# Making S5's parameters in three pieces, after the first token block instead of within it

## The chip, the cores and the metric

The kernel runs on one core of a Trainium2 chip. The metric is the device time of one execution in microseconds (us); smaller is better. Engines are named as the profile names them: PE is TensorE (PEld its weight loads), DVE is VectorE, ACT is ScalarE, POOL is GpSimd, SP is SyncE, which issues nearly all of this kernel's DMAs in the order of its queue.

## What is computed

One inference step of a two-layer recurrent decoder over a prompt of 2048 tokens and 8 single-token samples, model width 1024, all in float32. The first, even layer matters here. It projects the normed input once; some of the columns go to 4 heads of gated linear attention (GLA), the others to 32 groups of a complex-diagonal state space model (S5). Both results are gated, concatenated and projected back. S5's discretised parameters depend on weights alone:

```python
def s5_scan(u, h0_re, h0_im, lam_re, lam_im, log_dt, b_re, b_im, c_re, c_im, d):
    dt = jnp.exp(log_dt)[:, None]
    mag = jnp.exp(lam_re * dt)
    ar, ai = mag * jnp.cos(lam_im * dt), mag * jnp.sin(lam_im * dt)
    den = lam_re * lam_re + lam_im * lam_im
    wr = ((ar - 1.0) * lam_re + ai * lam_im) / den
    wi = (ai * lam_re - (ar - 1.0) * lam_im) / den
    ...
def even_mixer(h, s_gla, s_re, s_im, ...):
    q, k, v, r, lr, u, sg = jnp.split((h @ w_in).astype(f32), _offsets(EVEN_SIZES), axis=-1)
    ...
    o, s_gla_new = gla_chunked(q, k, v, log_a, s_gla.astype(f32))
    o = rmsnorm(o, gla_norm_w).reshape(bsz, L, GLA_V_WIDTH) * jax.nn.silu(r)
    y5, h_re, h_im = s5_scan(u, s_re.astype(f32), ...)
    ...
    out = jnp.concatenate([o, y5], axis=-1).astype(h.dtype) @ w_out
```

The second, odd layer (a gated delta rule) and the final norm follow; the change doesn't touch them.

## The kernel before

Tokens are worked in four blocks of 512 for GLA (the first also holds the 8 samples) and in two halves for S5. For each block GLA runs an entry (transposes, norm, split of the input into a high and a low part), then per head the dense products (`gla_dense`, 6 projections of 128 columns, three passes each), a prefix of decays (`gla_prefix`), a chain over the four chunks (`gla_chain`) with a gate (`gla_gate`), in the first block a sample step (`gla_sample`), and at the end of the block the output projection (`gla_out`), whose sums are added to the residual on VectorE (line 1064). In the first block the weights come as raw rows and are split by ScalarE and GpSimd (lines 319, 320) and stored; later blocks load the stored halves.

S5's preparation runs beside that. `s5_params` (from line 383) loads three small weight rows, transposes them on TensorE, and makes on VectorE with [128, 32] operations (helper on line 389): the angle reduced to a sine and cosine (two ScalarE activations, lines 436 and 437), nine powers of the complex step, three squarings, and the multiples of the angle, 16 fine (`rb`) and 9 coarse (`ra`). All lie in one tile Q of 68 columns for each of 32 groups, stored by one DMA (line 511) to the DRAM tensor s5q. `s5_state` (line 1078) loads the samples' S5 states in 8 steps into the tile hr, transposes each on TensorE into h0s, and stores h0s. `s5_tables` makes one group's tables from its row of s5q (32 times, about 18 us each, small products on VectorE and GpSimd, two products on TensorE) and stores them in DRAM for the S5 stage.

The order on TensorE is written out: `Weave.run` gives each stream its turn by a planned time, the modelled time of TensorE. A stream yields either so many planned us (`yield LAT["far"]`, 8 us) or an event that another stream posts. TensorE executes in that order, whether the data is there or not. The other engines' order is the scheduler's, in which a stream's lead counts. `s5_make` is the stream of S5's preparation, and has no lead, like the dense streams; chains, prefixes and samples have one.

SBUF places are pools that open and close as stacks on two sides. Before the change `start` (S5's parameters) is open on the right side from the first, and `out2`, which holds GLA's Oh and Ol tiles, opens only after it closes. The event "o0", posted with the first Oh and Ol tiles, lets the first block's gates and samples go on. After `out2` the pool `tabs` opens for the tables, then `ext`, with two more residual buffers. The event ("gtail", 0) is posted when the dense products of the first block's four heads are all issued; the output projection of that block and the entry of the second wait for it, the entry also for the last sample's step. The S5 stage itself waits for the end of all GLA chains and for the tables.

A tile's tag names its place, and a tag with one buffer is reused in turn: a new tile waits until the last reader of the old one, a DMA too, is done.

Of the kernel before, what the change touches and what calls it, by code (L numbers as in the profile page):

```python
# [12 lines left out]
F32 = mybir.dt.float32  # L13
# [5 lines left out]
OP = mybir.AluOpType  # L19
# [4 lines left out]
P = 128  # L24
# [3 lines left out]
NSM = 8  # L28
# [12 lines left out]
           inv4=0.837, inv5=0.796, inv6=0.972, chain1=0.972, chain2=0.729, chain3=0.837, split=1.95, sload=2.66,  # L41
           cout=2.25, norm=5.5, load=2, us=3.74, sq=4, out=3.24, entry=9.6, x=1.88, gentry=7.98, make=30, far=8,
           pr=1.5, gate=9, lvl1=4.73, lvl=1.8, gnorm=6.8, scan=2.33, tab=10, entry5=8, glu=3, gelu=1.5, ysum=6)
# [96 lines left out]
def tile_trunk(ctx, tc, A, O):  # L140
# [244 lines left out]
    def s5_params(st):  # L385
# [4 lines left out]

        temps, tiles = {}, []

        def rt(name):
            k = len(temps) % 8
            if k == 0:
                tiles.append(st.tile([P, 8, SG], F32, tag="rt", bufs=2, name="rt"))
            temps[name] = tiles[-1][:, k]
            return temps[name]

        Q = st.tile([P, SG, NQ], F32, tag="Q", name="Q")  # L400
        cut = lambda a, n: Q[:, :, a:a + 2 * n].rearrange("p g (i n) -> p i n g", i=2)
        pw = cut(0, SR + 1)
        ra, rb = cut(RA, 9), cut(RB, 16)
        rows = st.tile([SG, 3, P], F32, tag="rows", name="rows")
        for h in range(2):
# [19 lines left out]
        lre, lim, dtb = prm[:, 0], prm[:, 1], prm[:, 2]  # L425
        th, kk, mag, t0, t1, t2, t3 = [rt(x) for x in ("th", "kk", "mag", "t0", "t1", "t2", "t3")]
        sn, cs, rden, am1 = [rt(x) for x in ("sn", "cs", "rden", "am1")]
        vtt(t0, lre, dtb, OP.mult)
# [51 lines left out]
        x0 = st.tile([P, 7, SG], F32, tag="rows", name="x0")  # L480
        x1 = st.tile([P, 7, SG], F32, tag="x1", name="x1")

# [6 lines left out]

        for r, top in ((rb, 16), (ra, 8)):  # L490
            nc.gpsimd.memset(r[:, 0, 0], 1.0)
            nc.gpsimd.memset(r[:, 1, 0], 0.0)
            at = lambda n: (r[:, 0, n], r[:, 1, n])
            n = 1
            while n < top:
                if n > 1:
                    m = n - 1
                    cb, sb = [x.unsqueeze(1).to_broadcast([P, m, SG]) for x in at(n)]
                    c_, s_ = r[:, 0, 1:n], r[:, 1, 1:n]
                    vtt(x0[:, :m], c_, cb, OP.mult)  # L500
                    vtt(x1[:, :m], s_, sb, OP.mult)
                    vtt(r[:, 0, n + 1:2 * n], x0[:, :m], x1[:, :m], OP.subtract)
                    vtt(x0[:, :m], c_, sb, OP.mult)
                    vtt(x1[:, :m], s_, cb, OP.mult)
                    vtt(r[:, 1, n + 1:2 * n], x0[:, :m], x1[:, :m], OP.add)
                n *= 2
                square((ra[:, 0, 1], ra[:, 1, 1]) if n == 16 else at(n), at(n // 2))
# [818 lines left out]
    def s5_glu(sp, half):  # L1326
# [64 lines left out]
        if ns:  # L1391
# [10 lines left out]
    sp = Phase(tc, "s5", early=("Hh", "Hl", "h0"), entry=("xb", "rr"),  # L1402
               start=("Q", "rt", "rows", "ldt", "ev", "dt", "drow", "prm", "x0", "x1", "h0s", "hr"),
               tabs=("q", "kp", "pp", "v0", "v1", "bx", "by", "cx", "cy", "xx", "xy", "y1", "y2", "dd", "smI", "smC", "smR"),
# [4 lines left out]
    sp.pools["out"] = gp.pools["out"]  # L1409
    sp.open("start", "right")  # L1410
    gp.open("main", "left")
# [81 lines left out]
    def s5_make():  # L1493
        yield LAT["make"]
        yield from s5_params(sp)
        yield from s5_state()
        sp.close("start")
        gp.open("out2", "right")
        sp.pools["out2"] = gp.pools["out2"]
        og_[GBLK[0]] = gla_o()  # L1500
        weave.post("o0")
        sp.open("tabs", "right")
        for g in range(SG):
            yield from s5_tables(sp, g)
        sp.close("tabs")
        gp.open("ext", "right")
        weave.post("tabs")
# [833 lines left out]
```

## Time and profile before

| | us |
|---|---|
| median of 3 runs | 3261.68 (3260.92 to 3266.36) |
| the profiled execution's own time | 3250.56 |
| its span | 3248.8 |
| TensorE busy | 2955.9 (91%) |
| VectorE busy | 2224.4 (68%) |
| ScalarE busy | 1255.7 (39%) |
| GpSimd busy | 995.0 (31%) |
| DMA, queue of SyncE | 57.3% of 16 engines' span |

The profile is one execution; the profiled execution's own time is 11.1 us below the median of the timed runs. The page cuts the span in 40 slices, and from slice 7 on TensorE is busy for nine tenths or nearly so. To see a stage, a table of stretches is read: busy time of each engine in a window, the clock granted to TensorE as a share of 2.4 GHz, and the share of time that the 16 DMA engines were busy. The window less the busy time is idle time, and the list of waits says on which instruction each idle time ended.

### The profile page before, as it was taken

The numbers are of one execution on the slowest core, as the hardware profiler recorded it, in microseconds if no ns is written. First come the engines' busy times: TensorE is split into PE (matmuls) and PEld (weight loads), VectorE is DVE, ScalarE is ACT, GpSimd is POOL, SyncE is SP. The second block draws the span as 40 slices with busy tenths as digits, with TensorE's granted clock in tenths as the row PEclk, the third lists the DMA queues.
The fourth block names the chain that finished last, engine by engine and source line by source line (L and its number), as shares of the span: only waits on it lengthen the run. The fifth ranks groups of instructions, "written<-read, shape, count | busy, mean of one in ns | idle before, by whom it ended". The sixth has DMA issues, their size and how long they took to land.

```text
span 3248.8 us, 53026 instructions
## 1 busy us (share of the span) xinstructions
PE 2955.9 (91%) x18425; PEld 2497.5 (77%) x18425; DVE 2224.4 (68%) x5715; ACT 1255.7 (39%) x3321; POOL 995.0 (31%) x1236
## 2 busy tenths in 40 slices
PE   6888799999999989978988888899998999999998
PEld 5877678777778768877767888877887788787886
DVE  7766556645444546765867888867887678857885
ACT  5443343323323323241134444443444344434442
POOL 6565444322202222240034444431112121211111
PEclk8898899999999999989999999999999999999999
DMA  7565965673483485664466566676444844475446
GB/s 216 190 209 177 297 184 148 190 256 126 136 276 126 133 287 153 200 202 148 155 198 216 172 193 185 190 230 221 139 147 140 270 146 145 125 234 192 141 139 191
DMA packets 398232, 602.96 MB, mean 186 GB/s; under 512 B 62521, under 2 KB 257964, under 8 KB 397828
## 3 DMA queue, kind: packets, MB, share of 16 engines
q1 hardware_dynamic: 394902, 589.98, 57.3%
q0 software_dynamic: 2560, 8.42, 0.9%
q8 instruction: 145, 2.38, 0.3%
q10 hardware_dynamic: 502, 1.17, 0.1%
q14 instruction: 123, 1.01, 0.1%
HBM read 433.31 MB, written 166.34 MB: 185 GB/s over the span
## 4 chain that ended last, share of the span: by engine, by line
PE 35%; DVE 15%; DMA 4%; issue 3%; ACT 2%; POOL 1%; SPq 0%; POOLq 0%; DVEq 0%; ACTq 0%
PE pmm L93 23%; PE prc L93 5%; PE ptp L97 2%; PE pch L93 2%; DVE yc L1692 2%; PE ppo L93 2%; DVE z L1237 1%; DVE z L1247 1%; DVE Hl L649 1%; DMA out<-yt 1%; DMA LB<-md_d 1%; DVE z L1243 1%; DMA whl<-split 1%; DVE z L1238 0%; DVE z L1248 0%
## 5 line engine op out<-in xcount | busy, mean ns | idle before, releaser
L93 PE MATMUL pmm<-Hh,whl 128*128 128x512 f32 (+4 forms) x5200 | 1597.3, 370 | 42.8 <-ACT pre L1682 13.2
L93 PEld LDWEIGHTS pmm<-Hh,whl 128*128 128x128 f32 x5200 | 951.2, 193 | 173.8 <-ACT pre L1682 14.8
L93 PE MATMUL pmm<-Hl,whl 128*128 128x512 f32 (+5 forms) x2640 | 937.0, 355 | 5.6 <-DVE Hl L649 4.2
L93 PEld LDWEIGHTS pmm<-Hl,whl 128*128 128x128 f32 (+1 forms) x2640 | 506.5, 192 | 55.6 <-DVE Hl L649 6.0
L93 PE MATMUL pmm<-Oh,whl 128*128 128x512 f32 (+2 forms) x1120 | 354.3, 379 | 30.5 <-DVE res L1064 13.4
L320 POOL TENSOR_TENSOR whl<-raw,whl 128x512 fp32r<-128x512 f32 (+1 forms) x176 | 232.3, 1322 | 203.9 <-ACT whl L319 194.9
L93 PEld LDWEIGHTS pmm<-Oh,whl 128*128 128x128 f32 x1120 | 211.3, 200 | 65.7 <-DVE res L1064 16.9
L1692 DVE SCALAR_TENSOR_TENSOR yc<-pre,cvec,yc 128x512 f32<-128x512 f32 (+1 forms) x288 | 228.8, 795 | 43.2 <-ACT yc L1690 40.5
L93 PE MATMUL pmm<-Ol,whl 128*128 128x512 f32 (+2 forms) x560 | 203.3, 363 | 0.6 <-DVE Ol L370 0.6
L319 ACT ACTIVATE whl<-raw 128x512 fp32r<-128x512 f32 (+1 forms) x176 | 108.5, 618 | 127.4 <-PE pmm L93 78.0
L93 PEld LDWEIGHTS pmm<-Ol,whl 128*128 128x128 f32 x560 | 112.6, 201 | 11.4 <-DVE Ol L370 1.7
L907 DVE TENSOR_TENSOR dlt<-b 128x512 f32<-128x512 f32 x112 | 87.5, 782 | 39.8 <-ACT E L914 38.9
L93 PE MATMUL pmm<-oh,whl 128*128 128x512 f32 (+3 forms) x320 | 93.6, 370 | 18.3 <-DVE res L1378 15.4
L908 ACT ACTIVATE E<-dlt 128x256 f32<-128x256 f32 x112 | 47.4, 423 | 156.1 <-DVE dlt L907 32.3
L1682 ACT ACTIVATE pre<-pmm 128x512 f32<-128x512 f32 (+1 forms) x120 | 61.1, 510 | 115.4 <-PE pmm L93 115.1
L646 POOL TENSOR_TENSOR xb<-xb,rr 128x1024 f32<-128x1024 f32 (+1 forms) x32 | 76.9, 2412 | 90.9 <-DMA xb<-xs_d 40.4
L1968 ACT ACTIVATE jk<-ppo,rq 128x128 bf16<-128x128 f32 x128 | 46.7, 365 | 140.2 <-PE ppo L93 139.1
L1685 POOL COPY halo<-pre 128x3 f32<-128x3 f32 x96 | 22.3, 232 | 241.0 <-ACT pre L1682 240.3
L1064 DVE TENSOR_TENSOR res<-pmm,res 128x512 f32<-128x512 f32 (+2 forms) x80 | 46.2, 584 | 68.6 <-PE pmm L93 50.0
L1729 ACT ACTIVATE jk<-ptp 128x128 bf16<-128x128 f32 x256 | 70.8, 277 | 53.8 <-PE ptp L97 48.3
L275 POOL TENSOR_TENSOR s<-s,mhalf 128x4 f32<-128x4 f32 (+2 forms) x41 | 40.6, 989 | 162.6 <-DVE s L274 160.7
L1695 ACT ACTIVATE th<-yc 128x512 f32<-128x512 f32 (+1 forms) x96 | 61.0, 635 | 73.1 <-DVE yc L1692 72.8
(1527 smaller groups left out, 6103.8 us busy)
## 6 DMA issues: line engine op xcount, KB each, us to landing
whl<-split SPq DMA_DIRECT2D x460, 512.0 KB
split<-whl SPq DMA_DIRECT2D x168, 512.0 KB
res<-xs_d SPq DMA_DIRECT2D x88, 256.0 KB
sm<-s5m SPq DMA_DIRECT2D x32, 514.0 KB
raw<-in_w_in_even SPq DMA_DIRECT2D x64, 256.0 KB
xs_d<-res SPq DMA_DIRECT2D x64, 256.0 KB
raw<-in_w_in_odd SPq DMA_DIRECT2D x64, 256.0 KB
LB<-md_d SPq DMA_DIRECT2D x64, 256.0 KB
```

What stands on the lines that cost most here:

```text
L93: return self.e.matmul(out, w, x, **kw)
L97: return self.e.transpose(out, x, ident)
L319: nc.scalar.activation(t[:, 0, :m], raw, AF.Copy)
L320: nc.gpsimd.tensor_tensor(t[:, 1, :m], raw, t[:, 0, :m].bitcast(F32), op=OP.subtract)
L646: nc.gpsimd.tensor_tensor(xb, xb, rr.unsqueeze(1).to_broadcast(list(xb.shape)), op=OP.mult)
L907: nc.vector.tensor_tensor(d3, b3, b3[:, :, s - 1:s].to_broadcast([P, nb_, 2 * s]), op=OP.subtract)
L908: nc.scalar.activation(E3[:, :, s:], d3[:, :, s:], AF.Exp, scale=IS)
L1682: nc.scalar.activation(pre[:, X0 + c * P:X0 + (c + k) * P], ps[:, n0:], AF.Copy)
L1692: nc.vector.scalar_tensor_tensor(yv, pre[:, i:W - 3 + i], convw[:, ti, i:i + 1], yv, op0=OP.mult, op1=OP.add)
L1695: nc.scalar.activation(t[:, 3:W], yv, AF.Tanh, scale=0.5)
L1729: nc.scalar.activation(jk, pt[:, c * P:(c + 1) * P], AF.Square, accum_out=ss[:, c:c + 1])
L1968: nc.scalar.activation(jk[:rows], po[:rows, c * P:(c + 1) * P], AF.Square, scale=rq[:rows, c:c + 1], accum_out=s1[:, c:c + 1])
```

## The change

The parameters are no longer made at 30 planned us but when the first block's dense products have been issued, in the place where the tables lie afterwards. `out2` opens at the start of the kernel and "o0" is posted at once. To fit, the tile Q becomes three pieces in two tags, and hr and h0s take the same two tags:

- tag qb: the nine powers (18 columns), then the coarse multiples `ra` (18 columns), then h0s
- tag qa: the loaded weight rows, then the fine multiples `rb` (32 columns), then hr

Each piece is stored by its own DMA to its columns of s5q. The temporaries share one tile, the multiples are made in steps of at most four instead of up to seven, and the last squarings go to `cs` and `sn` and are copied into the pieces.

```diff
     def s5_make():
-        yield LAT["make"]
+        og_[GBLK[0]] = gla_o()
+        weave.post("o0")
+        yield "gtail", 0
+        sp.open("start", "right")
         yield from s5_params(sp)
         yield from s5_state()
         sp.close("start")
-        gp.open("out2", "right")
-        sp.pools["out2"] = gp.pools["out2"]
-        og_[GBLK[0]] = gla_o()
-        weave.post("o0")
         sp.open("tabs", "right")
...
     gp.open("out", "right")
     sp.pools["out"] = gp.pools["out"]
-    sp.open("start", "right")
+    gp.open("out2", "right")
+    sp.pools["out2"] = gp.pools["out2"]
...
     def s5_state():
-        h0 = sp.tile([P, 2, SG, NSM], F32, tag="h0s", bufs=1, name="h0s")
+        h0 = sp.tile([P, 2, SG, NSM], F32, tag="qb", bufs=1, name="h0s")
...
-                hr = sp.tile([NSM, 8, 2, SP], F32, tag="hr", bufs=1, name="hr")
+                hr = sp.tile([NSM, 8, 2, SP], F32, tag="qa", bufs=1, name="hr")
...
     def s5_params(st):
...
-        Q = st.tile([P, SG, NQ], F32, tag="Q", name="Q")
-        cut = lambda a, n: Q[:, :, a:a + 2 * n].rearrange("p g (i n) -> p i n g", i=2)
-        pw = cut(0, SR + 1)
-        ra, rb = cut(RA, 9), cut(RB, 16)
-        rows = st.tile([SG, 3, P], F32, tag="rows", name="rows")
+        def piece(tag, n):
+            t = st.tile([P, SG, 2 * n], F32, tag=tag, name="Q")
+            return t, t.rearrange("p g (i n) -> p i n g", i=2)
+        rows = st.tile([SG, 3, P], F32, tag="qa", name="rows")
...
+        Qw, pw = piece("qb", SR + 1)
...
-            vtt(rb[:, 0, 1] if it == 2 else cs, t0, t1, OP.subtract)
-            V.tensor_scalar(rb[:, 1, 1] if it == 2 else sn, t2, 2.0, None, op0=OP.mult)
+            vtt(cs, t0, t1, OP.subtract)
+            V.tensor_scalar(sn, t2, 2.0, None, op0=OP.mult)
             vtt(rho if it == 2 else mag, mag, mag, OP.mult)
+        nc.sync.dma_start(s5q[:, :, :RA], Qw)
+        Qb, rb = piece("qa", 16)
+        V.tensor_copy(rb[:, 0, 1], cs)
+        V.tensor_copy(rb[:, 1, 1], sn)
...
-        for r in (ra, rb):
-            V.tensor_scalar(r[:, 1], r[:, 1], sgn, None, op0=OP.mult)
-        nc.sync.dma_start(s5q, Q)
+        eighth = multiples(rb, 16)(8)
+        square((cs, sn), eighth)
+        V.tensor_scalar(rb[:, 1], rb[:, 1], sgn, None, op0=OP.mult)
+        nc.sync.dma_start(s5q[:, :, RB:], Qb)
+        Qa, ra = piece("qb", 9)
+        V.tensor_copy(ra[:, 0, 1], cs)
+        V.tensor_copy(ra[:, 1, 1], sn)
+        multiples(ra, 8)
+        V.tensor_scalar(ra[:, 1], ra[:, 1], sgn, None, op0=OP.mult)
+        nc.sync.dma_start(s5q[:, :, RA:RB], Qa)
```

## Rows read from the trace of the kernel before

**Rows 1.** Stretches of the even layer: window, busy us of five engines, clock, DMA, GB/s.

```profile
39.00:130.00 91.00, 75.47 (x533) 71.62 (x532) 74.67 (x235) 43.68 (x87) 53.85 (x40) 0.85 0.54 174
130.00:317.00 187.00, 159.34 (x1157) 140.01 (x1157) 127.28 (x278) 78.11 (x195) 120.11 (x155) 0.93 0.61 194
317.00:413.00 96.00, 74.84 (x490) 66.67 (x491) 54.88 (x156) 29.58 (x76) 36.94 (x63) 0.88 0.91 292
413.00:615.00 202.00, 198.84 (x1058) 158.37 (x1057) 129.50 (x309) 76.97 (x183) 94.93 (x164) 1.00 0.54 161
615.00:692.00 77.00, 65.53 (x279) 48.04 (x278) 44.95 (x125) 18.69 (x52) 18.35 (x43) 0.93 0.86 274
...
885.00:950.00 65.00, 57.99 (x254) 43.73 (x253) 34.07 (x79) 14.83 (x36) 3.10 (x5) 0.97 0.78 242
```

**Rows 2.** TensorE's waits, 39 to 130 us: on whom, us in total, times, longest.

```profile
PE ptp L97 <- POOL kt L887: 5.0, 1, 5.0
PE pmm L93 <- DVE rsil L819: 2.6, 1, 2.6
PE ppo L93 <- DVE pt L961: 2.3, 1, 2.3
...
PE prc L93 <- DVE rt L389: 2.1, 1, 2.1
```

**Rows 3.** TensorE's waits, 130 to 317 us.

```profile
PE ppo L93 <- DVE pt L961: 5.5, 1, 5.5
...
PE ptp L93 <- DVE smC L523: 4.3, 1, 4.3
...
PE ptp L97 <- DVE h0s L1093: 1.0, 1, 1.0
```

**Rows 4.** TensorE's waits, 317 to 413 us.

```profile
PE pmm L93 <- DVE res L1064: 9.2, 5, 3.6
PE pmm L97 <- DVE res L1064: 7.2, 1, 7.2
PE pmm L93 <- DVE kp L523: 4.2, 1, 4.2
```

**Rows 5.** VectorE groups, 39 to 117 us; then line 389 (ns min/median/max, first, last start).

```profile
L389 DVE TENSOR_TENSOR Q<-rt 128x32 f32<-128x32 f32 x24 | 11.7, 503 | 2.6 <-POOL rt L429 2.6
...
L389 DVE TENSOR_TENSOR rt<-Q x49: 182/205/1287, 51.3 to 107.9; 128x32 f32<-128x32 f32 x49
```

**Rows 6.** Timeline of TensorE: start, us, engine, line, operation, count [idle before].

```profile
38.47 0.52 PE L97 MATMUL ptp<-ident,rows 32*128 32x32 f32 x3
...
49.90 0.66 PE L97 MATMUL ptp<-ident,hr 8*128 8x8 f32 x8
...
317.04 0.39 PE L93 MATMUL pmm<-Oh,whl 128*128 128x264 f32 x1 [1.14 <-DVE rsil L819]
```

**Rows 7.** Timeline of VectorE: parameters' copy, the cosine, the multiples' sign.

```profile
39.08 0.26 DVE L423 COPY prm<-ptp 128x96 f32<-128x96 f32 x1 [2.35 <-PE ptp L97]
...
50.71 0.18 DVE L439 TENSOR_SCALAR rt<-rt 128x32 f32<-128x32 f32 x1
...
108.32 0.67 DVE L510 TENSOR_SCALAR Q<-Q,sgn 128x512 f32<-128x512 f32 x1
```

**Rows 8.** Line 389 alone, a stretch: window, VectorE busy us, clock, DMA, GB/s.

```profile
50.00:109.00 59.00, 33.08 (x117) 0.83 0.56 178
```

**Rows 9.** The store of Q on the page; SyncE's queue, 448 to 451 us: packets, MB, share.

```profile
s5q<-Q SPq DMA_DIRECT2D x1, 1088.0 KB
...
q1 hardware_dynamic: 1104, 0.54, 68.3%
```

**Rows 10.** Table loads, table stores, GLA state updates: ns min/median/max, first to last start.

```profile
L528 SPq DMA_DIRECT2D q<-s5q x32: 319/382/1127, 129.9 to 669.6; - x32
...
L629 SPq DMA_DIRECT2D s5m<-smI x32: 319/336/1910, 172.0 to 708.9; - x32
...
L983 DVE SCALAR_TENSOR_TENSOR gS<-gS,ebl,pch x64: 459/479/483, 112.1 to 1163.2; 128x256 f32<-128x256 f32 x64
```

More of the change, by code (lines that the diff above doesn't have):

```diff
@@ L41 @@
            inv4=0.837, inv5=0.796, inv6=0.972, chain1=0.972, chain2=0.729, chain3=0.837, split=1.95, sload=2.66,
-           cout=2.25, norm=5.5, load=2, us=3.74, sq=4, out=3.24, entry=9.6, x=1.88, gentry=7.98, make=30, far=8,
+           cout=2.25, norm=5.5, load=2, us=3.74, sq=4, out=3.24, entry=9.6, x=1.88, gentry=7.98, far=8,
            pr=1.5, gate=9, lvl1=4.73, lvl=1.8, gnorm=6.8, scan=2.33, tab=10, entry5=8, glu=3, gelu=1.5, ysum=6)
@@ L389, in vtt @@
             V.tensor_tensor(o, a, b, op=op)
[L391 to L398, printed above, removed]
-        Q = st.tile([P, SG, NQ], F32, tag="Q", name="Q")
-        cut = lambda a, n: Q[:, :, a:a + 2 * n].rearrange("p g (i n) -> p i n g", i=2)
-        pw = cut(0, SR + 1)
-        ra, rb = cut(RA, 9), cut(RB, 16)
-        rows = st.tile([SG, 3, P], F32, tag="rows", name="rows")
+        names = ("mag", "t0", "t1", "t2", "t3", "sn", "cs", "th", "kk")
+        rt_ = st.tile([P, len(names), SG], F32, tag="rt", name="rt")
+        rt = lambda name: rt_[:, names.index(name)]
+        def piece(tag, n):
+            t = st.tile([P, SG, 2 * n], F32, tag=tag, name="Q")
+            return t, t.rearrange("p g (i n) -> p i n g", i=2)
+        rows = st.tile([SG, 3, P], F32, tag="qa", name="rows")
         for h in range(2):
@@ L425, in s5_params @@
         lre, lim, dtb = prm[:, 0], prm[:, 1], prm[:, 2]
-        th, kk, mag, t0, t1, t2, t3 = [rt(x) for x in ("th", "kk", "mag", "t0", "t1", "t2", "t3")]
-        sn, cs, rden, am1 = [rt(x) for x in ("sn", "cs", "rden", "am1")]
+        mag, t0, t1, t2, t3, sn, cs, th, kk = [rt(x) for x in names]
+        rden, am1 = th, kk
+        Qw, pw = piece("qb", SR + 1)
         vtt(t0, lre, dtb, OP.mult)
@@ L478, in s5_params @@
         V.tensor_scalar(wv[:, 1], wv[:, 1], sgn, None, op0=OP.mult)
-        x0 = st.tile([P, 7, SG], F32, tag="rows", name="x0")
-        x1 = st.tile([P, 7, SG], F32, tag="x1", name="x1")
+        x0 = st.tile([P, 4, SG], F32, tag="x0", name="x0")
+        x1 = st.tile([P, 4, SG], F32, tag="x1", name="x1")
         def square(d, e):
@@ L488, in square, with multiples @@
             V.tensor_scalar(d[1], t2, 2.0, None, op0=OP.mult)
-        for r, top in ((rb, 16), (ra, 8)):
+        def multiples(r, top):
             nc.gpsimd.memset(r[:, 0, 0], 1.0)
@@ L495, in s5_params @@
             while n < top:
-                if n > 1:
-                    m = n - 1
+                for a in range(1, n, 4):
+                    m = min(4, n - a)
                     cb, sb = [x.unsqueeze(1).to_broadcast([P, m, SG]) for x in at(n)]
-                    c_, s_ = r[:, 0, 1:n], r[:, 1, 1:n]
+                    c_, s_ = r[:, 0, a:a + m], r[:, 1, a:a + m]
                     vtt(x0[:, :m], c_, cb, OP.mult)
                     vtt(x1[:, :m], s_, sb, OP.mult)
-                    vtt(r[:, 0, n + 1:2 * n], x0[:, :m], x1[:, :m], OP.subtract)
+                    vtt(r[:, 0, n + a:n + a + m], x0[:, :m], x1[:, :m], OP.subtract)
                     vtt(x0[:, :m], c_, sb, OP.mult)
                     vtt(x1[:, :m], s_, cb, OP.mult)
-                    vtt(r[:, 1, n + 1:2 * n], x0[:, :m], x1[:, :m], OP.add)
+                    vtt(r[:, 1, n + a:n + a + m], x0[:, :m], x1[:, :m], OP.add)
                 n *= 2
-                square((ra[:, 0, 1], ra[:, 1, 1]) if n == 16 else at(n), at(n // 2))
-        for r in (ra, rb):
-            V.tensor_scalar(r[:, 1], r[:, 1], sgn, None, op0=OP.mult)
-        nc.sync.dma_start(s5q, Q)
+                if n < 16:
+                    square(at(n), at(n // 2))
+            return at
+        eighth = multiples(rb, 16)(8)
[8 more added lines that the diff above has]
+        nc.sync.dma_start(s5q[:, :, RA:RB], Qa)
     GB = 2
@@ L1402, in tile_trunk @@
     sp = Phase(tc, "s5", early=("Hh", "Hl", "h0"), entry=("xb", "rr"),
-               start=("Q", "rt", "rows", "ldt", "ev", "dt", "drow", "prm", "x0", "x1", "h0s", "hr"),
+               start=("qa", "qb", "rt", "ldt", "ev", "dt", "drow", "prm", "x0", "x1"),
                tabs=("q", "kp", "pp", "v0", "v1", "bx", "by", "cx", "cy", "xx", "xy", "y1", "y2", "dd", "smI", "smC", "smR"),
```

## The prediction

> **What bounds the kernel now.** Start with the page's slices: TensorE is busy 88 to 100% nearly everywhere, and its first six slices are the exception. So I cut the recurrent even layer into its stages and read one table of stretches [rows 1]. The reader should compare the first token block (39 to 317 us) with the second (413 to 615 us). Block one leaves TensorE idle for 91 - 75.5 = 15.5 us and 187 - 159.3 = 27.7 us, 43.2 us in all; block two leaves 202 - 198.8 = 3.2 us. The granted clock tells the same: 0.85 and 0.93 of full speed against 1.00. A mean of 0.85 says that 30% of that stretch ran at 1.2 GHz instead of 2.4, so of its busy time 0.15 x 75.5 = 11.3 us is loss, and in the next stretch 0.07 x 159.3 = 11.2 us. Block one therefore holds 43 + 22.5, some 66 us that block two doesn't have. That is the most that any relief of block one can give.
>
> Then I read who ends TensorE's waits [rows 2, 3]. Four carry the mark of S5's parameters: one waits directly on a parameter temporary (2.1), two on VectorE results queued between parameter operations (2.6 and 2.3), and one on ke, GpSimd's product for the first prefix (5.0), which is late because VectorE stood behind the parameters' power and sine. In the second stretch smC (4.3) is a table's product and h0s (1.0) the state's copy. Together 17.3 us. The rest are samples, prefixes and weights that the change leaves where they are.
>
> Last, the seam between block one and block two, 317 to 413 us: 21.2 us idle, clock 0.88, DMA share 0.91. Its waits end on the output projection's residual add [rows 4], and the first is a table's (kp, 4.2).
>
> **The change, part by part.** *Parameters out of block one.* They are 158 VectorE instructions in 27 groups, 48 us together, of which [rows 5] shows the largest and the range of one instruction. They ran while VectorE was 82% busy (74.7 of 91 us, [rows 1]). The tables of block one, some 10 of 32 at 18 us each (below), go with them, and so do their GpSimd products. What comes back: the 17.3 us named, and of the other 26 us a third, 8.6, because VectorE and GpSimd are lighter for the samples; together 26 us of idle. Low clock follows idle gaps in these stretches, so I return it in proportion: 26/43 x 22.5 = 13 us. Sum: 39 us. The lower bound is the parameters' and tables' own waits with half the ke and pt ones, 13.7 us, and 4 of clock: 18. The upper bound is block two's level: 43 + 22.5 - 3.2 = 62. I take 39, near the middle: samples and raw weights stay, but both ends of their waits are VectorE and GpSimd, which are relieved.
>
> *The Oh/Ol tiles from the start.* The gates and samples of block one no longer wait until the sample states are transposed. I cost that at nothing: the dense products cover it, and without them it would have shown as one long gap, while the longest is 5.0 us [rows 2].
>
> *More instructions.* Splitting the seven-wide step adds 6 products, and the pieces add 4 copies: 10 x 0.2 = 2 us on VectorE, hidden in the wait below.
>
> *The parameters at the seam.* Here the change adds a wait. S5's sample states are loaded into hr, which until now had a tile of its own. Now hr takes the tag of rows and then of the second piece, with one buffer. So the first hr load, on SyncE's queue, must wait until that piece is computed and stored. But TensorE's order is written out by planned time: params' transposes 2 us after the first block's products end, hr's transposes 8 us after that, whether the data is there or not. In the kernel before the two were 11.4 us apart, and hr was there [rows 6]. After the change TensorE reaches hr's transposes some 14 us after the seam begins and stands until the load lands. Behind it in TensorE's queue are the output projection of block one, the last head's chain, the fourth sample's products and the second block's entry, which waits for that sample.
>
> How long? Let S be the seam's start. Before, transposes to the cosine took 38.5 to 50.9, 12.4 us [rows 6, 7], with two ScalarE sines and a GpSimd power on the way; so S + 15. From the cosine to the second piece's end took 50.9 to 109.0, 58 us [rows 7]; but VectorE was shared then. The parameters' own products were 33 us of it [rows 8], some of them at up to 1.3 us against a median of 0.2 [rows 5]. With TensorE standing, less competes: I take 25 us (bounds 18 and 45), so S + 40. Then the store. Before it was one transfer of 1088 KB [rows 9], contiguous on both sides. Now it is three that write runs of 72, 128 and 72 bytes, 128 x 32 = 4096 packets each. The nearest row is a stretch full of small reads: 1104 packets at 68.3% of 16 engines over 3 us, 30 ns each [rows 9]. An estimate from it: 4096 x 30 ns / 16 = 7.7 us a piece. Then hr itself, 2 to 3 us: S + 51. TensorE stands from S + 14 to S + 51, 37 us; with VectorE at its bounds and the packets at half or twice 30 ns, 25 to 65 us.
>
> Not all of it is added. The seam's own 21.2 us was made by late loads and adds. While TensorE stands, residuals and weights land and no table runs: the 4.2 us of kp and half of the 16.4 us of res [rows 4] go, 12 us. The clock is as low as before, so no term. Net at the seam: 37 - 12 = +25 us (bounds +8 and +55).
>
> The Trainium skill speaks against the three stores: DMA: Bandwidth & Descriptors, section Specifications, gives 512 bytes as the smallest transfer at line rate and says that below it the engine reads, modifies and writes. No row of this trace has such small writes, and the small reads above neither bear it out nor speak against it. If a store so takes twice its time, an estimate by that page, the data comes some 15 us later and the forecast below becomes about 3267; that is most of the way to rival A, which holds it.
>
> *Tables later.* From the first table's load at 129.9 us to the last one's store at 708.9 the 32 tables take 579 us [rows 10]. They would start near 430 and end near 1010, while the last state update of this stage was at 1163.2 [rows 10]. That leaves 150 us before anyone waits for them. In steady blocks they cost nothing that can be seen: 3.2 us idle with them. Only the third seam gets them anew. The seam with tables was idle for 77 - 65.5 = 11.5 us, the one without for 65 - 58 = 7.0 [rows 1]. That is +4 us (0 to 8), and the two extra residual buffers that open when the tables end, a block later now, are in that figure.
>
> **Sum.** -39 + 25 + 4 = -10 us against the profiled execution's 3250.56 us (span 3248.8): 3241. The median of the three timed runs, 3261.68, lies 11.1 us above the profiled one, so the same shift gives 3252.
>
> **Rivals.** *A: the wait at the seam is longer than what block one gives back.* Its place is hr's first transpose, its price the time until the second piece is stored. It decides from a wait of 37 + 10 + 6.5, about 54 us. It gets there if VectorE works through the parameters as crowded as before (45 us instead of 25: 20 us more), or if the 72-byte writes cost much more than 30 ns. With both, the sum is -39 + 55 + 4 = +20: 3282. For it: the order on TensorE is fixed, and the tag is shared without doubt. Against it: with TensorE standing there is little else for VectorE to do.
>
> *B: the wait hardly bites.* If TensorE comes to hr late, since output tiles wait for VectorE behind the parameters anyway, or the parameters need only VectorE's lower bound and the stores half of 30 ns a packet, the seam costs +8, and block one gives 45: -45 + 8 + 4 = -33, 3229.
>
> *C: block one is bound by its samples and by splitting the raw weights.* Then only the named waits leave, 17.3 us and 6 of clock: -23 + 25 + 4 = +6, 3268. For it: the largest wait of the second stretch, pt 5.5 [rows 3], ends on neither parameters nor tables. Against it: VectorE and GpSimd are both relieved there.
>
> **How the numbers follow.** A measurement of this kernel can tell about 0.2%, 6.5 us, from no change: 3255 to 3268. Forecast, -30 to +5 around 3252: 0.42, of which 0.28 lies faster and 0.14 within. A: 0.28, all but 0.02 slower. B: 0.17, faster. C: 0.13, 0.06 within and 0.07 slower. Faster 0.45, within 0.22, slower 0.33. B's far end (62 from block one, +8, 0: 3208) and A's far end (-18 + 55 + 8: 3307) are both unlikely; leaving a tenth on each side gives 3220 to 3288. As cases of both signs hold weight, the likeliest one's own range: 3232 to 3266.
>
> **What would show it.** The first output-projection product, now at 317.0 us [rows 6], should come at 270 to 285, with block one's idle near 17 us and clock above 0.93. A gap of 25 to 65 us on TensorE should stand just before hr's first transposes, ended by the hr load. hr's load should follow the second piece's store by a few us. Tables should run from about 430 to 1010 us, and the even layer's end should not wait for them. The forecast is wrong if there is no such gap (B), if it passes 54 us (A), or if block one's end moves by less than 25 us (C). After 1165 us the traces should run alike, only shifted.

## The result

The changed kernel takes 3282.45 us (median of 6, 3276.5 to 3287.8) against 3259.86 (median of 6) of the kernel before on the same chip: a ratio of 1.0079, 95% interval 1.0059 to 1.0098. It is slower by 22.6 us by the medians, 26 by the ratio. The forecast was 3252, a little faster; the time is that of rival A, 3282.

The profiled execution of the changed kernel has a span of 3284.0 us, 35.2 more than the one of before. Of that, 12.6 us is chance: before's profiled execution was a quick one (below its median by 9 us), after's is 3 us above its own. Where a stage is told below, it is by these two executions.

First the stretches of the changed kernel that answer to [rows 1]; the columns are the same.

```profile
39.00:119.00 80.00, 67.66 (x501) 62.91 (x500) 41.57 (x63) 40.18 (x83) 41.98 (x38) 0.93 0.61 197
119.00:283.00 164.00, 146.21 (x1093) 134.51 (x1094) 97.14 (x184) 73.38 (x178) 85.54 (x74) 0.94 0.59 191
283.00:416.00 133.00, 74.84 (x527) 67.00 (x526) 71.71 (x286) 29.19 (x70) 29.52 (x30) 0.79 0.78 203
416.00:633.00 217.00, 203.79 (x1056) 160.85 (x1054) 131.41 (x306) 77.55 (x182) 89.69 (x155) 0.96 0.50 149
```

Block one now ends at 283 instead of 317; the seam takes 133 us instead of some 95, at a clock of 0.79; block two takes 217 instead of some 200. What fills the seam is one line of TensorE's waits there (us in total, times, longest), the answer to [rows 4]:

```profile
PE ptp L97 <- DMA hr<-in_state_s_im: 43.6, 1, 43.6
PE pmm L93 <- DVE rsil L831: 5.6, 1, 5.6
PE pmm L93 <- DVE res L1076: 2.4, 2, 2.1
PE pmm L97 <- DVE res L1076: 1.9, 1, 1.9
```

And here is how it comes about. The timelines of TensorE, VectorE and SyncE (SPq, its DMA issues) in the seam, each in its own order; they answer to [rows 6] and [rows 7]:

```profile
295.25 0.41 PE L97 MATMUL ptp<-ident,rows 32*128 32x32 f32 x3
348.34 0.99 PE L97 MATMUL ptp<-ident,hr 8*128 8x8 f32 x8 [43.59 <-DMA hr<-in_state_s_im]
...
306.61 0.17 DVE L436 TENSOR_SCALAR rt<-rt 128x32 f32<-128x32 f32 x1
325.54 0.28 DVE L519 COPY Q<-rt 128x32 f32<-128x32 f32 x1 [4.18 <-DMA s5q<-Q]
330.88 0.69 DVE L516 TENSOR_SCALAR Q<-Q,sgn 128x512 f32<-128x512 f32 x1
334.77 0.53 DVE L522 TENSOR_SCALAR Q<-Q,sgn 128x288 f32<-128x288 f32 x1
...
315.11 0.62 SPq L472 DMA_DIRECT2D s5q<-Q  x1
331.59 0.53 SPq L517 DMA_DIRECT2D s5q<-Q  x1
335.32 0.51 SPq L523 DMA_DIRECT2D s5q<-Q  x1
340.84 0.48 SPq L1098 DMA_DIRECT2D hr<-in_state_s_re  x1
```

TensorE reaches hr's transposes at 348.34 - 43.59 = 304.75. By then the cosine is not yet made. The second piece is ready at 331.6, its store holds the place until 340.84, and hr's load, now behind the third piece's store, lands at 348.3. Meanwhile TensorE stands, with the whole seam behind it in its queue.

By stages, the difference of the two executions (first output product of a block to the end of its projection, and so on):

| stage | length before | after | TensorE idle before | after |
|---|---|---|---|---|
| block one's products, from 39 us | 278.0 | 244.2 | 41.9 | 29.9 |
| seam | 95.2 | 132.6 | 22.3 | 58.0 |
| block two's products | 199.3 | 216.9 | 3.2 | 13.2 |
| from there to the last output product | 587.2 | 593.9 | 33.1 | 35.0 |
| the rest of the kernel | 2050.0 | 2057.3 | | |

(Lengths are differences of the starts of the first and last products of each stage in TensorE's timeline; idle is the sum of its gaps there.) -33.8 + 37.4 + 17.6 + 6.7 + 7.3 = +35.2. The last term is not the change's: in the stretch of the odd layer that shows it, the same work ran at another granted clock (first row before, second after),

```profile
1800.00:2000.00 200.00, 175.65 (x1545) 165.88 (x1544) 171.65 (x505) 91.95 (x294) 89.80 (x96) 0.97 0.59 185
...
1828.00:2028.00 200.00, 174.12 (x1458) 163.76 (x1457) 162.67 (x479) 87.38 (x276) 84.40 (x91) 0.91 0.56 174
```

and the profiled executions below, whose code is the same there too, show anything from 0.91 to 0.97 in it. Over the last 2050 us of the span, cut into windows of 50 us, the part of TensorE's busy time that low clock took (busy time times one less the clock) sums to 49 us before and 57 after, and to 47 to 63 in the others. So executions of this kernel differ by 7 us and more after 1200 us, whatever is done ahead of it.

### The profile page after: what moved, and what is told of

The parts are those of the page before. It is cut to its first block, busy times and chain, and to the rows that moved or that the text cites. A ratio compares the mean times of both kernels' runs of the same rounds, so it can differ in the third digit from the quotient of the medians.

```text
span 3284.0 us, 53071 instructions
## 1 busy us (share of the span) xinstructions
PE 2954.6 (90%) x18425; PEld 2496.1 (76%) x18425; DVE 2213.2 (67%) x5725; ACT 1252.4 (38%) x3320; POOL 987.8 (30%) x1236
## 4 chain that ended last, share of the span: by engine, by line
PE 34%; DVE 15%; DMA 5%; issue 3%; ACT 2%; POOL 2%; SPq 0%; POOLq 0%; DVEq 0%; ACTq 0%
PE pmm L93 23%; PE prc L93 5%; PE ptp L97 2%; PE pch L93 2%; PE ppo L93 2%; DVE yc L1704 1%; DVE z L1249 1%; DVE z L1259 1%; DMA LB<-md_d 1%; DMA xb<-xs_d 1%; DVE Hl L661 1%; DVE z L1255 1%; DMA out<-yt 1%; DMA whl<-split 1%; DVE z L1250 0%
## 5 line engine op out<-in xcount | busy, mean ns | idle before, releaser
L93 PEld LDWEIGHTS pmm<-Ol,whl 128*128 128x128 f32 x560 | 109.8, 196 | 11.1 <-DVE Ol L370 1.2
L920 ACT ACTIVATE E<-dlt 128x256 f32<-128x256 f32 x112 | 47.4, 424 | 152.5 <-DVE dlt L919 33.8
```

Source lines behind the costliest of these rows:

```text
L93: return self.e.matmul(out, w, x, **kw)
L920: nc.scalar.activation(E3[:, :, s:], d3[:, :, s:], AF.Exp, scale=IS)
```

## The experiments

Two questions: is it the wait for hr that turns the sign, and why did block one give back less than forecast. In the table, "block one ends" is the first output product, idle is TensorE's, ratios are to the kernel before on the same chip with the 95% interval. The kernels were timed in several sets and on more than one chip (the kernel before's median lay between 3256.3 and 3259.9 in them), so two medians of different sets are compared by their ratios too, and where medians and ratios disagree the size of the difference is open. In the six kernels with the state first (e6, e8, e11, e12, e13, e15) a gap of up to 3.3 us between the last product of the seam and hr's last transposes counts with the seam; in e10 a gap of 3.4 us at that place, on a residual, counts with block two.

| kernel | median us | ratio | block one ends | idle, seam | idle, block two |
|---|---|---|---|---|---|
| before | 3259.86 | 1 | 317.0 | 22.3 | 3.2 |
| changed | 3282.45 | 1.0079 (1.0059 to 1.0098) | 283.2 | 58.0 | 13.2 |
| e1 state late | 3254.86 | 0.9993 (0.9975 to 1.0011) | 285.8 | 39.7 | 4.0 |
| e2 whole stores | 3268.06 | 1.0035 (1.0016 to 1.0054) | 280.7 | 43.0 | 11.2 |
| e3 early | 3301.22 | 1.0121 (1.0088 to 1.0153) | 359.4 | 20.0 | 9.6 |
| e4 early, state late | 3259.80 | 1.0007 (0.9989 to 1.0025) | 330.3 | 14.9 | 6.2 |
| e5 late and whole | 3252.98 | 0.9985 (0.9973 to 0.9998) | 281.1 | 26.4 | 9.5 |
| e6 state first | 3246.49 | 0.9960 (0.9944 to 0.9977) | 277.9 | 16.8 | 21.6 |
| e7 steady | 3252.31 | 0.9993 (0.9976 to 1.0009) | 280.0 | 16.9 | 18.4 |
| e9 steady, whole | 3251.47 | 0.9980 (0.9966 to 0.9994) | 282.5 | 17.0 | 17.3 |
| e12 first, whole | 3236.64 | 0.9946 (0.9925 to 0.9967) | 281.3 | 17.8 | 10.4 |
| e8 first, halved tile | 3233.64 | 0.9933 (0.9915 to 0.9952) | 270.4 | 15.1 | 21.4 |
| e13 first, whole, halved | 3224.68 | 0.9896 (0.9881 to 0.9912) | 268.4 | 15.2 | 10.7 |
| e10 before, halved tile | 3258.29 | 0.9996 (0.9979 to 1.0013) | 318.7 | 17.0 | 6.4 |
| e11 first, no sample product | 3240.79 | 0.9959 (0.9940 to 0.9977) | 275.2 | 16.6 | 22.2 |
| e14 changed, halved tile | 3273.66 | 1.0049 (1.0032 to 1.0066) | 273.8 | 58.2 | 13.8 |
| e15 first, no sample update | 3221.18 | 0.9880 (0.9860 to 0.9900) | 258.0 | 11.1 | 20.6 |

Kernels whose block one is the changed kernel's word for word end it anywhere between 277.9 and 285.8 us (eight kernels, 281.6 on average); smaller differences there mean nothing.

### The wait for hr

**e1, state late.** The state's loads and transposes come 50 us of planned time after the parameters.

```diff
         yield from s5_params(sp)
+        yield 50.0
         yield from s5_state()
```

> The changed kernel with one more turn: 50 planned us between the parameters and the first load of the sample states, so that TensorE comes to hr's transposes later. Theory W (the wait of 43.6 us on hr, seen in the changed kernel, is the loss, and block one keeps its gain of some 21 us): the gap is gone, some 8 us of idle at the seam come back, net -36 us, 3247 against 3282, which is faster than before by about 12. Rival D (the parameters' own load on VectorE and the stores' on the DMA engines cost the seam so much anyway, and the gap only covers idle that returns in another place): 3275 to 3290, and the seam's idle stays near 58 us, spread over many waits. First output product at 283 us in both.

The gap at hr is gone and the time is that of before: 27.6 us (3282.45 to 3254.86) hung on that wait. But the 3247 that theory W named isn't reached, as the seam still has 39.7 us of idle, now on residuals. VectorE's timeline has the reason, and so has SyncE's queue:

```profile
368.81 0.42 DVE L1076 TENSOR_TENSOR res<-pmm,res 128x256 f32<-128x256 f32 x1 [11.63 <-DMA res<-xs_d]
...
353.69 0.94 SPq L523 DMA_DIRECT2D s5q<-Q  x1
354.72 7.38 SPq L1074 DMA_DIRECT2D res<-xs_d  x1
```

The residual's load is issued right behind the third small store and its issue alone takes 7.4 us, where the same line's others in this seam take 0.3 to 1.3 (the residual's store right behind the first small store took 4.7); VectorE stands 11.6 us for it, and TensorE behind VectorE.

**e2, whole stores.** Each piece gets a DRAM tensor of its own and is written in one run per partition; the tables load from three.

```diff
-        nc.sync.dma_start(s5q[:, :, :RA], Qw)
+        nc.sync.dma_start(s5qw, Qw)
...
-        nc.sync.dma_start(t, s5q[:, g])
+        nc.sync.dma_start(t[:, :RA], s5qw[:, g])
+        nc.sync.dma_start(t[:, RA:RB], s5qa[:, g])
+        nc.sync.dma_start(t[:, RB:], s5qb[:, g])
```

> The changed kernel with each of the three pieces stored whole into a DRAM tensor of its own, and each table's load made of three. In the changed kernel's trace VectorE stood 4.2 us for the first store, hr's load was issued 9.2 us after the second store, and landed 7 us later, behind the third store: 20 of the 43.6 us. Theory W with slow stores: the stores take 2 to 3 us each, the gap falls to about 28 us, the time by some 14, to 3268. If the gap is made of VectorE's work alone: it falls by 5 us at most, and the time stays within 5 us of 3282. Theory D: 3282, whatever the gap does.

```profile
PE ptp L97 <- DMA hr<-in_state_s_im: 27.3, 1, 27.3
```

The gap shrinks by 16.3 us and the time by 14.4, as the theory of slow stores said: the small packets were over a third of the wait.

**e3, early.** The parameters start 30 us of planned time in, as near to before's place as the new order allows; pieces and shared places stay.

```diff
-        yield "gtail", 0
+        yield 30.0
```

> The changed kernel with the parameters back at 30 planned us, in block one, but with the pieces, the shared tags and the Oh/Ol tiles from the start as in the change. Theory W: hr's transposes stand at about 50 us in TensorE's order, and the second piece is ready only about 90 to 110 us with VectorE as crowded as there; a gap of 40 to 55 us, first output product at about 350 us, time 3295 to 3310. Theory D (a wait on hr is covered by what would be idle anyway): within 10 us of the kernel before, 3250 to 3270.

```profile
PE ptp L97 <- DMA hr<-in_state_s_im: 53.8, 1, 53.8
```

The same gap, longer, in block one itself (ending at 103.1 us), where VectorE is crowded. So the wait comes from the shared place and goes wherever the parameters go.

**e4, early and state late.** Both edits together: what the new form costs in the old place.

> The same as the one with the parameters at 30 planned us in block one, and 50 planned us more between the parameters and the first load of the sample states. No gap on hr. What is left against the kernel before is the pieces and their small stores and the Oh/Ol tiles from the start: theory W says 3260, within 8 us. The difference to the kernel with the same 50 us at the seam is then what the move alone is worth: 13 us by W; near zero, or the other sign, by D.

3259.8, no different from before, as W said. Against e1 the move of place alone is worth 5 us, where W had 13 and D nothing; the intervals of the two ratios overlap, so it can't be told from nothing. Of what block one gains (it ends at 285.8 instead of 330.3), the seam takes back over half (39.7 of idle instead of 14.9). In this kernel block one ends 13 us later than in the kernel before, with a wait of 12.4 us for a table's load (cx) that no forecast named, and the seam is the shorter by some 10.

**e5, late and whole.** e1 and e2 together.

> Both repairs at the seam at once: the state's hr loads 50 us of planned TensorE time after the parameters, and the three stores whole (one DRAM tensor each). Late state alone left 39.7 us of TensorE idle at the seam (285.8 to 399.4 us), and there VectorE stands 11.6 us for a residual load that was issued behind the second and third piece's 4096-packet stores, and 2.0 us for the first store. Theory S (what is left of the loss at the seam is the small-packet stores holding up other transfers): the idle falls by 12 to 14, to about 26 us, and the time to about 3242, 0.4% under the kernel before. Rival V (it is the parameters' 33 us of VectorE work, whose place in its queue is ahead of the residual adds): the idle stays at 35 or more and the time within 3250 to 3258.

The idle of the seam falls as theory S said, from 39.7 to 26.4: of 31.8 us of waits on residuals 12.7 were the stores'. The time falls by less, to 0.9985 of before: 5.0 of the 13 us come back in block two as a wait for a table's load (cx), as in the changed kernel (6.0). That wait stands here although the stores are whole, so the small packets aren't its cause.

**e6, state first.** The state's eight steps, 8 planned us each, come before the parameters, whose transposes so run at 382.6 us, 105 us after block one's products, when block two has begun.

```diff
-        yield from s5_params(sp)
         yield from s5_state()
+        yield from s5_params(sp)
+        yield 60.0
```

> The state's step runs ahead of the parameters instead of behind them, still beside block two on. hr then never waits for a parameter piece; instead the first parameter rows wait for the last hr to be read, and the first piece for the store of the state's tile. Theory W (the order, that is who holds the shared tag first, decides, not the sharing): no gap of over 10 us at hr, nor one at the parameters' transposes, because 60 us of planned time lie between; the time is that of the late state, 3250 to 3260. Rival (sharing costs whichever comes first): a gap of 15 to 40 us at the parameters' transposes and 3270 to 3290.

Only 2.7 us are left ahead of hr's last transposes, and 1.9 at the parameters'. At 0.9960 it is the first that is faster than before by more than the 0.2% that the prediction calls telling. The sharing itself costs next to nothing if the long-lived holder, whose end hangs on a chain of VectorE work and stores, comes second. But this kernel also begins the parameters some 100 us later, so its 8 us (11 by the ratios) over e1 aren't shown to be the order's. What is left stands in block two, whose waits are

```profile
PE pch L93 <- DVE gS L995: 12.0, 2, 10.2
PE ppo L93 <- DVE pt L973: 6.5, 1, 6.5
```

and VectorE's own line there,

```profile
453.53 0.22 DVE L535 TENSOR_TENSOR u<-bx,wv 128x64 f32<-128x64 f32 x1 [8.18 <-DMA bx<-in_s_b_re]
```

says why gS is late: the first table's operation stands ahead of it in VectorE's queue, waiting for its load. SyncE's queue says why that load is late:

```profile
435.53 0.51 SPq L523 DMA_DIRECT2D s5q<-Q  x1
...
450.14 0.33 SPq L540 DMA_DIRECT2D q<-s5q  x1
```

The load of a table's row of s5q must wait until the third small store has landed, 14.6 us after that store's issue (6.9 us of it the queue stands idle), and the loads of bx are issued behind it.

**e7 and e9, steady.** The parameters begin with block two's first head, with the state late; e9 with whole stores too.

```diff
-        yield "gtail", 0
+        yield "gentry", 1
...
         yield from s5_params(sp)
+        yield 50.0
         yield from s5_state()
```

> Late state as before, and the parameters begin not at the end of block one's products but when block two's first head may begin, so that their VectorE work and their small stores fall into block two's steady stretch, where before TensorE was idle for 3.2 of 202 us, VectorE busy 64% and the DMA share 0.54. Theory P (the seam is the wrong place: it has neither VectorE nor DMA to spare, the steady stretch has both): the seam's idle falls from 39.7 to 10 to 15 us (before's 22.3 less the tables' and half of the residuals' waits), block two gains 5 to 10 us of idle, and the time is 3232 to 3242, 0.5 to 0.8% under the kernel before. Rival Q (the parameters cost TensorE the same wherever they run, because its evictions stand behind them on VectorE): block two takes over the 18 us that the seam loses and the time stays at 3250 to 3258.

> The same as the run with the parameters in block two's steady stretch, with the three stores whole. Theory P: in a stretch with a DMA share of 0.5 the 12288 small packets, about 20 us of 16 engines, are hidden, so the time is within 4 us of that run. Rival S (the small stores block the loads that are issued behind them wherever they run): 8 to 14 us less than that run.

Theory P fails, and Q's time comes: the seam falls to 16.9, but block two rises by 15.2 over before, and the time is that of before by the ratio (0.9993). VectorE was busy 64% of that stretch in the kernel before [rows 1], and still the parameters cost TensorE there over half of what the seam lost. e9 lies 0.8 us under e7 by the medians, 4 by the ratios, whose intervals overlap: as P said of the stores, in the steady stretch they cost nothing that can be told. e7 and e6 have about the same idle in seam and block two (35.3 and 38.4) and differ by 6 us (11 by the ratios); why, stays open.

**e12, state first with whole stores.**

> State first and the three stores whole. With state first the parameters run from 382 to 436 us, in block two's first 70 us, where TensorE is idle 12.0 us for gS and 6.5 us for pt, and VectorE stands 8.2 us for a table's load. Theory S (that load is late because of the small-packet stores ahead of it): block two's idle falls from 21.6 to about 12 and the time by 8 to 12, to about 3236. Rival V (VectorE's parameter products crowd gS and pt): idle 18 or more, the time within 4 us of state first.

```profile
PE ppo L93 <- DVE pt L977: 4.3, 1, 4.3
PE pch L93 <- DVE gS L999: 4.1, 2, 2.3
```

S holds for the place: block two's idle falls from 21.6 to 10.4, and the 10.2 us wait for gS is gone with the small stores. For the time it isn't settled: 9.9 us less than e6 by the medians, but 4.6 by the ratios, whose intervals overlap.

### Block one

In the changed kernel the waits that the forecast had named are gone, and TensorE waits for others. Its waits from 39 to 283 us:

```profile
PE pch L93 <- DVE gS L995: 10.8, 3, 6.3
PE pmm L93 <- DVE rsil L831: 8.1, 4, 3.4
PE ptp L97 <- ACT vtmp L810: 4.6, 1, 4.6
PE ppo L93 <- DVE pt L973: 3.2, 1, 3.2
```

In the kernel before, from 39 to 317 us, the lines of gS and rsil were

```profile
PE pch L93 <- DVE gS L983: 5.3, 1, 5.3
...
PE pmm L93 <- DVE rsil L819: 2.8, 2, 2.6
```

Both end on VectorE, which is busy only 41.6 of the first 80 us. Its own waits say what it stands for: first the line of before (39 to 317 us), then that of after (39 to 283), then GpSimd's of both:

```profile
DVE sS L1029 <- POOL skv L1026: 11.0, 7, 4.2
...
DVE sS L1041 <- POOL skv L1038: 34.1, 13, 5.0
...
POOL skv L1026 <- DMA skv<-vs_d: 22.1, 10, 4.5
...
POOL skv L1038 <- DMA skv<-vs_d: 35.0, 12, 6.3
```

This is the samples' state update: a load of keys and values of two samples into one tile with one buffer, GpSimd's product, VectorE's two updates; then only may the next load begin. Without the parameters VectorE comes to each update sooner and stands there, with gS and rsil behind it; that is the reading which the next runs try.

**e8 and e10, the halved tile.** One sample a tile, two buffers, the same memory; e8 on top of state first, e10 on the kernel before.

```diff
-        for s in range(0, NSM, 2):
-            kv = gp.tile([P, 2, GDV], F32, tag="skv", bufs=1, name="skv")
+        for s in range(NSM):
+            kv = gp.tile([P, GDV], F32, tag="skv", bufs=2, name="skv")
```

> State first, and in addition the samples' key-value tile halved: one sample a tile in two buffers instead of two samples a tile in one, so the next load may run while VectorE still reads. In block one of the changed kernel VectorE stands 34 us, 13 times, for GpSimd's sample product (11 us in the kernel before), GpSimd in turn 35 us for that tile's load, and TensorE's waits on gS and rsil, 19 of its 30 us of idle, are VectorE's work behind these. Theory S (this chain of load, product and update is what block one runs into once the parameters are gone): block one's idle falls from 28 to 16 to 20 us, its clock rises by 0.02, and the time falls by 10 to 15 against state first, to 3232 to 3237. Rival R (GpSimd's splits of raw weights, 48 of 1.35 us, are the bound): idle stays at 25 or more and the time within 4 us of state first.

> The kernel before with the samples' key-value tile halved in the same way and nothing else. Theory S': there VectorE itself is the bound of block one's first stretch (82% busy, 11 us of waits for the sample product), so the sample chain is mostly covered: block one's idle falls by at most 5 of 42 us and the time stays within 3250 to 3262, not to be told from before. Rival (the sample chain costs the same with and without the parameters): 10 to 15 us less, 3243 to 3248.

e8 takes 12.9 us off e6 by the medians, as S said (8.8 by the ratios); but in the profiled executions block one ends only 7.5 sooner, with an idle that fell by 4.6 and not by 8 to 12 (28.1 to 23.5; the clock rose by 0.02 and 0.01). Another 5.7 lie in the seam, at a clock of 0.98 instead of 0.92, so part of the agreement may be chance. That block one does end sooner is clear from three kernels with the halved tile (e8, e13, e14: 268.4 to 273.8) against the eight without (277.9 to 285.8). The load is waited for still: from 39 to 270 us GpSimd stands 27 us for it, and VectorE 24 for GpSimd's product. So the single place is a part of the chain and not all of it. e10 changes nothing, as S' said: block one's idle is 41.9 with and without. The halved tile pays only where the parameters have gone.

**e11, no sample product.**

> State first, with GpSimd's product of the samples' keys and values left out (the state update takes the bare values), loads and the single buffer unchanged. It takes 14 products of 1.05 us from GpSimd in block one. Theory S (the load into the single buffer makes the chain): each round of load, product and update gets about 1 us of 9 shorter, block one's idle falls by 2 to 6 us and the time by 3 to 8 us against state first. Rival G (GpSimd's time is the bound): idle falls by 10 or more, the time by over 12.

The ratio is e6's to a ten-thousandth, 0.9959 (the median is 5.7 us lower). G falls by either; S's 3 to 8 us can't be told from nothing. VectorE now waits on the load directly:

```profile
DVE sS L1040 <- DMA skv<-vs_d: 35.9, 12, 4.7
```

So it is the load, with its single place as a part (e8), and not the time of GpSimd's product.

**e15, no sample update.**

> State first, with the whole update of the first layer's sample states left out (no load of the key-value tile, no product on GpSimd, no update on VectorE; the old states are used and stored). Theory S (samples hold block one): gS and rsil, 18 of 28 us of idle there, nearly go: idle falls to 8 to 14 us, clock to 0.97 or more in both stretches, block one ends 20 to 25 us earlier than with state first, at 253 to 258 us, and the time is 3220 to 3226. Rival R (raw weights' splits and the dense chain itself): the idle stays above 18 us and block one ends at 265 or later.

```profile
39.00:112.00 73.00, 65.06 (x503) 60.33 (x501) 34.24 (x59) 41.73 (x88) 39.60 (x34) 0.97 0.59 200
112.00:262.00 150.00, 143.59 (x1122) 133.51 (x1122) 80.89 (x162) 73.79 (x177) 77.81 (x64) 0.98 0.61 201
```

Block one ends 19.9 us earlier than in e6 (24 under the eight kernels' average), its idle is 14.1 (28.1), the rsil wait is 0.3 and gS 4.2; the seam is 10 us shorter, and the whole kernel takes 25.3 us less. The samples' update as a whole holds some 20 us of block one once the parameters are out, about what the forecast missed there (18). But with the load this run also takes VectorE's own updates away (it is busy 114 us of block one instead of 138), so it doesn't divide the 20 us between the wait for the load and that work.

**e14, the changed kernel with the halved tile.**

> The changed kernel as it is, with the samples' key-value tile halved into two buffers. Theory W plus S (two separate places: the samples' chain in block one, the wait for hr at the seam): the hr gap stays 42 to 46 us, block one ends 8 to 13 us earlier, and the time is 3268 to 3275, still slower than before. Rival (an earlier block one only lengthens the wait at the seam): gap 50 or more and time 3280 or more.

```profile
PE ptp L97 <- DMA hr<-in_state_s_im: 45.1, 1, 45.1
```

Two separate places: block one ends 9.4 us sooner, the gap stays, the time is 8.8 us less and still slower than before.

**e13, all three.**

> State first, whole stores and the halved sample tile together. If the three gains lie in different stretches (seam, block two, block one) they add: state first 0.9960, whole stores another 0.0014 to 0.0027, the halved tile another 0.0027 to 0.0039, so 0.990 to 0.992 of the kernel before, 3225 to 3231 us. Rival (the later one is hidden by the earlier, since the even layer's end is bound elsewhere): no better than either alone, 3233 to 3237.

3224.68 us, 0.9896 of the kernel before (0.9881 to 0.9912): the gains add, a little beyond what was expected. This version beats both kernels, by 34 and 58 us.

```profile
PE pmm L93 <- DVE res L1079: 6.8, 3, 5.6
PE pmm L93 <- DVE rsil L835: 3.4, 1, 3.4
PE ptp L97 <- DMA hr<-in_state_s_im: 3.3, 2, 2.9
```

These are its waits at the seam: what stood 43.6 us on hr now stands 3.3.

## Why the prediction was wrong

The mechanism at the seam was read rightly, and its size nearly. The sign was lost on three terms of the sum, each too kind by 8 to 18 us. That the time is rival A's to the microsecond is luck, as the end of the sum below shows.

**The largest: block one, -39.** The first output product came at 283.2, inside the 270 to 285 us that were to show the step right, but that was a poor mark, as it counts work that only moved; the other mark, idle near 17 us, failed with 29.9. TensorE's busy time from 39 us to it is 234.8 before [rows 1] and 213.9 after; with the part at low clock taken off (15% and 7%; 7% and 6%) 212 and 200, so 12 of the 33.8 us are transposes and tables' products that come later. What was gained is 12.0 of idle and 9 of clock, 21 us, not 39. The step that failed is "of the other 26 us a third, because VectorE and GpSimd are lighter", and with it the full return of the named 17.3: the named lines nearly all went, but gS rose from 5.3 to 10.8 and rsil from 2.8 to 8.1, as the samples' update became the limit (e15: 20 us with all of it gone). Rival C had that place and nearly that size: 17.3 + 6 = 23. Its argument against itself, that both engines are relieved, fails: VectorE stood 34.1 us for the samples' product instead of 11.0, and behind that product is a load (e11) whose single place is a part of it (e8). How much of the 20 us is the load and how much VectorE's own updates stays open.

**The wait: 37, measured 43.6.** From the start S = 283.2: cosine at S + 23 (forecast S + 15), as the transposes came 10 us later (5.6 of it the wait for rsil), and TensorE came to hr 7.5 later (S + 21.5 for S + 14), so that the two misses nearly cancel. From cosine to second piece 25.0 us, as forecast, with 4.2 of it VectorE's wait for the first store, which the forecast had not named; that it fits so well is in part luck. The second store 9.3 us for 7.7. And hr itself 7.5 for 2 to 3, since it queues behind the third store; that is the miss. A packet of the first store took about what was estimated (30 ns); from 315 to 325 us, with that store alone, the queue's packets, MB and share of 16 engines are

```profile
q1 hardware_dynamic: 4112, 0.29, 62.5%
```

10 x 0.625 x 16 / 4112 = 24 ns. The Trainium skill (DMA: Bandwidth & Descriptors, section Specifications) says that below 512 bytes the engine reads, modifies and writes; in this trace that does not show as twice the 30 ns of [rows 9], though that stretch of small reads had larger packets among them (862 of 1104 were under 512 bytes), and the factor of two was the prediction's own. What it says of 512 bytes as the least for line rate agrees: written whole, the second piece freed its place for hr within 2.7 us (e2) instead of 9.3.

**Less 12 us of seam idle.** 22.3 before, 58.0 - 43.6 = 14.4 beside the gap after: 7.9 went. kp's wait went and most of res; but 5.6 of rsil came, samples' work again (it is gone in e15). Net at the seam +35.7, forecast +25 (bounds 8 to 55). That the seam's clock needs no term held in effect: its mean fell from 0.88 to 0.79, but the stretch now is nearly half idle, and in pieces of some 12 us the busy time that low clock took is 8 us before and 6 after.

**Tables later: +4.** Block two has 10.0 us more idle, which the forecast had put at nothing ("in steady blocks they cost nothing that can be seen"): 6.0 is a wait for the first tables' load (cx; 0.5 in e1 and 0.8 in e2, but 5.0 in e5 and 6.3 in e9, both with whole stores, so the small packets don't decide it and its cause stays open), and 3.8 more is gS. The later stages have 1.9 more. So +11.9. That the tables end later (their last stores ran from 465 to 955 us; forecast 430 to 1010) did no harm at the even layer's end, which did not wait for them: that step held.

Summed up with what was measured: -21 + 35.7 + 11.9 = +27, against +27.9 of the two profiled executions up to the last output product, and +22.6 of the medians; the forecast's -10 differs by 18, 11 and 8. Left out of this sum is the clock behind the seam, which nearly cancels: block two's 0.96 for 1.00 costs about 8 us, the next stage's 0.99 for 0.98 gives about 5 back. By its own line rival A decides from a wait of 54 us; it came to pass at 43.6, because block one gave so little: A's outcome, C's reason.

**Two edits costed at nothing** held: Oh and Ol from the start (no gap in block one over 6.4 us) and the ten more VectorE instructions, hidden in the wait. That the traces run alike after 1165 us held for the idle, not for the clock (above).

## What to carry to other kernels

When work is taken off a crowded engine, ask which chain of load, product and update it will stand for next, and price that chain before crediting the relief: here the next one held 20 of some 40 us, and halving its tile gave nothing before the move and 9 to 13 us after it. When two tiles come to share a place, put first the one whose release needs only a load and a copy, and second the one whose release hangs on a long chain and a store; the order, with the later start that it gave the parameters, was worth 36 us here (3282 to 3246), and 28 of it came already with planning hr's transposes later (e1). A mark for a step must not count work that is only moved: compare busy time at full clock beside the end of the stage.

## What the runs showed of the hardware

Thousands of packets of 72 or 128 bytes cost more as a crowd than by their own transfer: 4112 took 24 ns each alone, but behind them the issue of a residual's load took 7.4 us on SyncE's queue (e1), and the third store, issued 4 us behind the second, landed only 14.6 us after its issue, so that VectorE's first table operation stood 8.2 us for the load behind it (e6). And the granted clock of the same odd-layer work differed from 0.91 to 0.97 between executions, and low clock took 47 to 63 us of the last 2050, so a single profiled execution can't settle a change of this size.
